# An encoder block in one program: the first norm's place in the engines' queues, weight rounding among bank copies, and a new cycle of weight-tile offsets

## The chip, the core and the metric

The kernel runs on one core of a Trainium2 chip. The core has a matrix engine (TensorE, PE in the profile; its weight loads are shown as PEld), a vector engine (VectorE, DVE), a scalar engine (ScalarE, ACT), GpSimd (POOL), and SyncE (SP), which here only issues transfers. Engines read and write the on-chip memory SBUF; TensorE adds up in PSUM, which has eight banks. Each engine takes its own instructions in order, and an instruction that needs another engine's result waits for a semaphore; what stands behind it waits too.

The metric is the device time of one execution in microseconds (us). The time before is 1913.99 us, the median of three runs (1913.49 to 1914.49).

## The reference

One layer on 256 tokens of width 2048, all in float32. Nine vectors (shift, scale and gate for three sublayers) come from one conditioning vector:

```
mod = silu(c) @ w_ada + b_ada;  sh1, sc1, gt1, sh2, ... = split(mod, 9)
h = h + 0.5 * gt1 * swiglu(rms_norm(h, g1) * (1 + sc1) + sh1, w1_gate, w1_up, w1_down)
qkv = (rms_norm(h, g2) * (1 + sc2) + sh2) @ w_qkv
h = h + gt2 * concat(rms_norm(natten(qkv)), rms_norm(dilated(qkv))) @ w_o
h = h + 0.5 * gt3 * swiglu(rms_norm(h, g3) * (1 + sc3) + sh3, w2_gate, w2_up, w2_down)
```

The two feed-forward parts have 5632 hidden columns. The mixing part has 16 heads of 128: eight with a 2-D neighbourhood, eight with three dilated windows.

## The kernel before, in words

Activations stand transposed: a tile has 128 of the 2048 features on the partitions and the 256 tokens along them. There are 16 such feature tiles, numbered k below.

**Weights.** All large weights are one stream of chunks of 128 x 1024 floats (0.5 MB), eight blocks of 128 x 128 in each, in the order in which TensorE needs them. A chunk is loaded into one of five raw buffers (`wraw`, tile `rw`). ScalarE rounds it to a reduced format (`wsplit`, tile `hiw`), and VectorE writes what the rounding left over (tile `low`). For each block TensorE then runs a pair of matmuls (`mm2`): the rounded weight against the activation's rounded part and its remainder together (512 columns), and the weight's remainder against the rounded part (256 columns). `hiw` and `low` have four buffers each, taken in turn. A buffer is 1024 + 64 floats long, and the constant `PLACE` says at which offset, counted in floats, chunk number n lies in it: entry n modulo 8 has the offset of `hiw` and that of `low`. The number n counts every chunk of the stream. The chunks of `w_qkv` lie at (0, 0) whatever `PLACE` says.

**The nine vectors.** `w_ada` is read in 144 pieces of 1 MB (tiles `ra` and `rx`, three buffers), and VectorE reduces each against silu(c) to one column of a vector (L144, 2.3 us). These pieces are spread over the kernel: `bg_step` issues one and uses an earlier one, and the weight stream calls it at a set number of pieces per chunk (`RA`, `RB` and so on).

**The start.** VectorE and TensorE spread silu(c) over the partitions (tiles `dg`, `pc`, `cb`), the squares of x are summed over the features by matmuls against ones (`sq1`, `pstat`), and `rstd_from` turns the sum into the norm's factor r by a logarithm, an exponential and one step of refinement. For each of the first K1 = 6 feature tiles, the scale and shift pieces are reduced, VectorE multiplies (`nt`), and ScalarE adds the shift, once in full float32 (`xf`) and once rounded (`nx`).

**The split part.** For these six feature tiles and the first eight hidden tiles (NF0), the weights (twelve chunks, `w1_s`) aren't split: TensorE multiplies them in full float32 against `xf` (L470), each of eight results in a bank of its own (`pa`). When a bank is complete, ScalarE copies it to SBUF (`park`, L348). Then `up_first` runs the remaining 24 hidden tiles over the same six feature tiles with split chunks (`w1_a`, 36 chunks), adding two halves on ScalarE and VectorE (L343, L344). The rest of the layer follows: `w1_b`, the down projections, attention, and the second feed-forward part.

**Order.** A recording layer places the instructions of ScalarE, VectorE and SyncE by its own estimate of when each can run; `tc.high_priority(offset=...)` moves what is written under it ahead in that choice, and `after` asks that one instruction stand behind another without a wait. TensorE's order is nearly that of the program text.

Of the kernel before, what the change touches and what calls it, by code (L numbers as in the profile page):

```python
# [9 lines left out]
F32 = mybir.dt.float32  # L10
F32R = mybir.dt.float32r
AF = mybir.ActivationFunctionType
ALU = mybir.AluOpType
AX = mybir.AxisListType

P = 128
S = 256
D = 2048
# [5 lines left out]
EPS = 1e-6  # L24
NEG = -1e30
CW = 1024
K1 = 6
# [21 lines left out]
URGENT = 400  # L49
SOON = 60  # L50
LINE = 16
PLACE = ((12, 36),) + 3 * ((16, 0),) + ((44, 40),) + 3 * ((48, 0),)
MANUAL = {mybir.EngineType.PE}


# [10 lines left out]
def build(tc, a):  # L66
    nc = tc.nc
    with ExitStack() as ctx:
        cp = ctx.enter_context(tc.tile_pool(name="cp", bufs=1))
# [4 lines left out]
        def psum_pool(kind):  # L74

            if "cm" in pools:
                pools.pop("cm").__exit__(None, None, None)
            if kind:
                pools["cm"] = tc.tile_pool(name=f"p{kind}", bufs=4 if kind == "pair" else 8,
                                           space=bass.MemoryType.PSUM, reuse_waits="tile")  # L80
                pools["p"] = pools["cm"].__enter__()
# [4 lines left out]
        def bank(nm):  # L86
            return pools["p"].tile([P, 512], F32, tag="b", name=nm)
# [2 lines left out]

        ones = cp.tile([P, P], F32, name="ones")
        nc.vector.memset(ones, 1.0)
        epst = cp.tile([P, 1], F32, name="epst")
        nc.vector.memset(epst, EPS)
        ident = cp.tile([P, P], F32, name="ident")
        make_identity(nc, ident)

# [4 lines left out]
        h4 = [cp.tile([P, 4, S], F32, tag=f"h{k}", name=f"h{k}") for k in range(4)]  # L102
# [11 lines left out]

        queue = []
        lows = []
        late = []

        def after(ins, other, why):
            tc.add_manual_dep(  # L120
                ins.ins, other.ins.name,
                mybir.DependencyInfo(mybir.DependencyClass.NoSync, mybir.DependencyReason.DATA),
                reason=why)
# [30 lines left out]
        def wraw(src):  # L154
            raw = wp.tile([P, CW], F32, tag="raw", bufs=RAWB, name="rw")
            ins = nc.sync.dma_start(raw, src)
            if ws.rate:
                queue[:] = [ins]
            return raw

        def wsplit(raw, place):
            hi = wp.tile([P, CW + 64], F32R, tag="whi", bufs=LOB, name="hiw")[:, place[0] : place[0] + CW]
            lo = wp.tile([P, CW + 64], F32R, tag="wlo", bufs=LOB, name="low")[:, place[1] : place[1] + CW]
            nc.scalar.copy(hi, raw)  # L164
            lows[:] = lows[-1:] + [nc.vector.tensor_tensor(lo, raw, hi.bitcast(F32), ALU.subtract)]  # L165
            return hi, lo

# [21 lines left out]
        def ln_exp_set():  # L189
            tc.keep_in_program_order(nc.scalar.preload_act_table_set("natural_log_exp_and_others"))  # L190

        def rstd_from(ps, n, w, tag):
            t0 = sp.tile([P, w], F32, tag="sq", name=f"{tag}0")
            t1 = sp.tile([P, w], F32, tag="nt", name=f"{tag}1")
            r = sp.tile([P, w], F32, tag=f"{tag}r", bufs=2, name=f"{tag}r")
            nc.scalar.activation(t0, ps, AF.Ln, scale=1.0 / n, bias=epst)
            nc.vector.tensor_scalar(t1, ps, -0.5 / n, -0.5 * EPS, ALU.mult, ALU.add)
            nc.scalar.activation(r, t0, AF.Exp, scale=-0.5)
            nc.vector.tensor_tensor(t0, r, r, ALU.mult)
            nc.vector.tensor_tensor(t0, t0, t1, ALU.mult)  # L200
            nc.vector.scalar_tensor_tensor(r, t0, 1.5, r, ALU.add, ALU.mult)
            return r

        class Stat:
# [25 lines left out]
            def rstd(self, n, tag="rs"):  # L230
                return rstd_from(self.ps, n, S, tag)

        def norm_mod(k, r, jsh, jsc, full=None):
            sh, gs = mods[jsh], mods[jsc]
            t = sp.tile([P, S], F32, tag="nt", name="nt")
            nc.vector.scalar_tensor_tensor(t, h[k], gs[:, k : k + 1], r, ALU.mult, ALU.mult)
            if full is not None:
                nc.scalar.activation(full, t, AF.Identity, bias=sh[:, k : k + 1])
            nc.scalar.activation(nx[k][:, 0, :], t, AF.Identity, bias=sh[:, k : k + 1])  # L239
            return nc.vector.scalar_tensor_tensor(  # L240
                nx[k][:, 1, :], t, sh[:, k : k + 1], nx[k][:, 0, :].bitcast(F32), ALU.add, ALU.subtract)
# [13 lines left out]
        def bg_use():  # L255
            raw, i, then = pend.pop(0)
            ada_use(raw, i)
            if then:
                then()

        def bg_step():
            i, then = bg.pop(0)
            while len(pend) >= (ARA + ARX - 1 if wide else ARA - 1):
                bg_use()
            pend.append((ada_issue(i), i, then))

        def bg_until(left):

            while len(bg) + len(pend) > left:
                if bg:  # L270
                    bg_step()
                else:
                    bg_use()
# [11 lines left out]
        srcs = []  # L285
        first = {}
        for nm in ("w1_s", "w1_a", "w1_b", "w1_d", "w1_c", "w1_e", "w_qkv", "w_o",
                   "w2_a", "w2_b", "w2_d", "w2_c", "w2_e"):
            first[nm] = len(srcs)
            for c in range(a[nm].shape[0]):  # L290
                srcs.append((a[nm][c], (0, 0) if nm == "w_qkv" else PLACE[len(srcs) % len(PLACE)]))

        class W:
# [8 lines left out]
            def fetch(self, n):  # L302
                while self.head < n:
                    self.ready[self.head] = wraw(srcs[self.head][0])
                    self.head += 1

            def whole(self):
                self.tail += 1
                return self.ready.pop(self.tail - 1)

            def chunk(self, ahead=AHEAD):
                while self.head <= min(self.tail + ahead, len(srcs) - 1):
                    self.ready[self.head] = wsplit(wraw(srcs[self.head][0]), srcs[self.head][1])
                    self.head += 1
                    self.credit += self.rate
                    while self.credit >= 1.0 and (bg or pend):
                        self.credit -= 1.0
                        if bg:
                            bg_step()
                        else:  # L320
                            bg_use()
                self.tail += 1
                return self.ready.pop(self.tail - 1)
# [13 lines left out]
        ws = W()  # L337
# [7 lines left out]

        def park(ps, f, part):
            part[f] = hp.tile([P, 2, S], F32, tag="hid", name=f"pt{f}")
            nc.scalar.copy(part[f], ps)  # L348

        def up_mm(ps, k0, k1, first, last):  # L350
            for j in range(2):
# [75 lines left out]
        part = {}  # L427
# [15 lines left out]
        ps1 = bank("pstat")[:, :S]  # L443
        for q in range(4):
            for i in range(2):
                sq = hp.tile([P, 2, S], F32, tag="hid", name="sq1")
                nc.scalar.activation(sq, h4[q][:, 2 * i : 2 * i + 2, :], AF.Square)
                nc.vector.tensor_tensor(sq[:, 0, :], sq[:, 0, :], sq[:, 1, :], ALU.add)
                nc.tensor.matmul(ps1, ones, sq[:, 0, :], start=q + i == 0, stop=q + i == 4)
        r1 = rstd_from(ps1, D, S, "rs")  # L450

        def first_full(k):
            full[k] = hp.tile([P, 2, S], F32, tag="hid", name=f"xf{k}")[:, 0, :]
            norm_mod(k, r1, 0, 1, full[k])

        full = {}
        for k in range(K1):
            bg_add((KT + k, k), lambda k=k: first_full(k))
        bg_pairs(K1, r1, 0, 1)
        pa = [bank(f"pa{f}").rearrange("p (j s) -> p j s", j=2) for f in range(NF0)]  # L460
        bg_step()
        bg_step()
        for k in range(K1):
            ws.fetch(2 * k + 2)
            bg_until((KT - 1 - k) * 2)
            for j in range(2):
                w = ws.whole()
                for b in range(8):
                    f, q = 4 * j + b // 2, b % 2
                    nc.tensor.matmul(pa[f][:, q, :], w[:, b * P : (b + 1) * P], full[k],  # L470
                                     start=k == 0 and q == 0, stop=k == K1 - 1 and q == 1,
                                     skip_group_check=True)
        for f in range(NF0):
            park(pa[f], f, part)
        psum_pool("pair")

        ws.pace(RA)
# [36 lines left out]
        with tc.tile_pool(name="att", bufs=2) as ap_, tc.tile_pool(name="atc", bufs=1) as ac:  # L514
# [41 lines left out]
            def qk_rstd(s_):  # L556
                s_["rr"] = rstd_from(s_["ss"], HD, 8, "rq")
# [197 lines left out]
        part = {}  # L755
# [103 lines left out]
def _program():  # L859
    import concourse.bacc as _bacc  # L860

    nc = _bacc.Bacc("TRN2", target_bir_lowering=False, num_devices=1, dynamic_dma_scratch_size=1024)
    aps = {k: nc.dram_tensor(f"in_{k}_dram", s, F32, kind="ExternalInput").ap() for k, s in _SHAPES.items()}
    aps["out"] = nc.dram_tensor("out_0_dram", (KT, P, S), F32, kind="ExternalOutput").ap()
    with tile.TileContext(nc) as tc:
        build(tc, aps)
    return nc
# [10 lines left out]
```

## Time and profile before

| What | Value |
|---|---|
| median of three timed runs | 1913.99 us |
| the profiled execution's own time | 1911.73 us |
| its span in the trace | 1910.0 us |
| TensorE busy | 1876.7 us, 98% |
| weight loads busy | 1633.8 us, 86% |
| VectorE busy | 1563.4 us, 82% |
| ScalarE busy | 907.5 us, 48% |
| granted TensorE clock, mean | 0.996 |
| read from HBM | 500.09 MB, 263 GB/s over the span |

The span runs from the first to the last instruction of the program; 1.7 us of the profiled execution lie around it. The busy share of TensorE says how long matmuls were under way and not how closely they follow each other, so the prediction also uses the length of stretches that hold a known number of matmuls. Times below are microseconds from the start of the span.

### The profile page before, as it was taken

What the parts mean: (1) busy time and instruction counts of PE and PEld (TensorE: products, weight loads), DVE (VectorE), ACT (ScalarE), POOL (GpSimd) and SP (SyncE); (2) the same over time, 40 slices, a digit from 0 to 9 for tenths busy, and PEclk for the clock granted to TensorE, in tenths of its full rate; (3) what the DMA queues carried; (4) which work ended last, traced back from release to release, by engine and by line L of the source; (5) the groups of instructions that cost most, each with busy time, mean ns of one, the idle gap of its engine ahead of it and who ended that gap; (6) DMA issues with size and microseconds to landing.
All of it is one profiled execution on the core that took longest, in us unless ns stands there. A gap on an engine that the chain in (4) does not pass through costs nothing.

```text
span 1910.0 us, 27533 instructions
## 1 busy us (share of the span) xinstructions
PE 1876.7 (98%) x10564; PEld 1633.8 (86%) x10564; DVE 1563.4 (82%) x2122; ACT 907.5 (48%) x1333; POOL 0.7 (0%) x6
## 2 busy tenths in 40 slices
PE   7999999999999999999999999999999999999999
PEld 5878888888888888888888888888888888888888
DVE  7899999988888889878887898888699985556565
ACT  2444544443334454555555555454555543334442
POOL 0000000000000000000000000000000000000000
PEclk8999999999999999999999999999999999999999
DMA  9988888889898987777765444888677876666664
GB/s 384 387 326 293 306 296 303 298 316 331 330 334 322 328 307 262 253 258 251 253 230 193 147 153 161 314 297 304 209 280 258 276 272 216 192 193 193 189 207 134
DMA packets 120227, 503.98 MB, mean 264 GB/s; under 512 B 13344, under 2 KB 15904, under 8 KB 101664
## 3 DMA queue, kind: packets, MB, share of 16 engines
q1 hardware_dynamic: 120096, 502.24, 75.4%
q8 instruction: 82, 1.34, 0.3%
q14 instruction: 49, 0.40, 0.1%
HBM read 500.09 MB, written 2.10 MB: 263 GB/s over the span
## 4 chain that ended last, share of the span: by engine, by line
PE 92%; DVE 5%; ACT 1%; DMA 1%; issue 1%; SPq 0%; ACTq 0%; DVEq 0%
PE pb L170 23%; PE pd L170 17%; PE pb L171 12%; PE pd L171 8%; PE pa L170 8%; PE pqk L176 5%; PE pqq L176 5%; PE pa L171 4%; PE pqv L176 4%; PE pa L470 2%; PE pso L170 2%; DVE low L165 2%; PE pso L171 1%; DVE ra L144 1%; DMA ra<-in_w_ada_dram 1%
## 5 line engine op out<-in xcount | busy, mean ns | idle before, releaser
L164 ACT CAST hiw<-rw 128x1024 fp32r<-128x1024 f32 x644 | 674.3, 1050 | 726.3 <-PE pd L170 241.7
L165 DVE TENSOR_TENSOR low<-rw,hiw 128x1024 fp32r<-128x1024 f32 x644 | 785.5, 1222 | 271.4 <-ACT hiw L164 269.8
L170 PE MATMUL pb<-nx,hiw 128*128 128x512 f32 x1920 | 656.8, 390 | 0.0
L171 PE MATMUL pb<-nx,low 128*128 128x256 f32 x1920 | 531.6, 277 | 0.7 <-DVE low L165 0.7
L170 PE MATMUL pd<-hd,hiw 128*128 128x512 f32 x1408 | 481.5, 390 | 0.0
L170 PEld LDWEIGHTS pb<-nx,hiw 128*128 128x128 f32 x1920 | 360.4, 188 | 76.6
L171 PE MATMUL pd<-hd,low 128*128 128x256 f32 x1408 | 389.6, 277 | 0.0
L171 PEld LDWEIGHTS pb<-nx,low 128*128 128x128 f32 x1920 | 360.5, 188 | 1.2 <-DVE low L165 1.2
L170 PEld LDWEIGHTS pd<-hd,hiw 128*128 128x128 f32 x1408 | 264.3, 188 | 56.2
L170 PE MATMUL pa<-nx,hiw 128*128 128x512 f32 x800 | 276.2, 392 | 4.7 <-ACT hiw L164 3.2
L171 PEld LDWEIGHTS pd<-hd,low 128*128 128x128 f32 x1408 | 264.3, 188 | 0.0
L144 DVE CUSTOM_DVE_ANT_0 ra<-ra,cb,vec 128x2048 f32<-128x2048 f32 x101 | 236.9, 2345 | 4.9 <-DMA ra<-in_w_ada_dram 4.9
L171 PE MATMUL pa<-nx,low 128*128 128x256 f32 x800 | 221.5, 279 | 3.9 <-DVE low L165 3.8
L170 PEld LDWEIGHTS pa<-nx,hiw 128*128 128x128 f32 x800 | 149.5, 188 | 38.5 <-ACT hiw L164 5.2
L171 PEld LDWEIGHTS pa<-nx,low 128*128 128x128 f32 x800 | 150.3, 188 | 8.8 <-DVE low L165 7.8
L144 DVE CUSTOM_DVE_ANT_0 rx<-rx,cb,vec 128x2048 f32<-128x2048 f32 x43 | 100.9, 2346 | 1.2 <-DMA rx<-in_w_ada_dram 1.2
L170 PE MATMUL pso<-ox,hiw 128*128 128x512 f32 x256 | 90.9, 399 | 0.0
L176 PE MATMUL pqk<-hiw,nx 128*128 128x512 f32 x256 | 84.3, 395 | 0.0
L176 PE MATMUL pqq<-hiw,nx 128*128 128x512 f32 x256 | 83.0, 393 | 0.0
L176 PE MATMUL pqv<-hiw,nx 128*128 128x512 f32 x256 | 81.4, 392 | 0.3 <-ACT nx L239 0.3
L385 DVE SCALAR_TENSOR_TENSOR h<-pd,m,h 128x256 f32<-128x256 f32 x128 | 60.8, 481 | 20.2 <-PE pd L171 18.3
L171 PE MATMUL pso<-ox,low 128*128 128x256 f32 x256 | 71.8, 280 | 0.0
(133 smaller groups left out, 1504.2 us busy)
## 6 DMA issues: line engine op xcount, KB each, us to landing
ra<-in_w_ada_dram SPq DMA_DIRECT2D x101, 1024.0 KB, 7.0
rw<-in_w_b_dram SPq DMA_DIRECT2D x144, 512.0 KB, 4.5
rw<-in_w_d_dram SPq DMA_DIRECT2D x128, 512.0 KB, 4.4
rw<-in_w_a_dram SPq DMA_DIRECT2D x100, 512.0 KB, 4.7
rw<-in_w_c_dram SPq DMA_DIRECT2D x96, 512.0 KB, 4.3
rw<-in_w_qkv_dram SPq DMA_DIRECT2D x96, 512.0 KB, 3.9
rx<-in_w_ada_dram SPq DMA_DIRECT2D x43, 1024.0 KB, 7.5
rw<-in_w_e_dram SPq DMA_DIRECT2D x48, 512.0 KB, 4.6
```

Of the source, the lines that this page charges most:

```text
L144: ins = nc.vector.tensor_tensor_reduce(out=raw, in0=raw, in1=cb, scale=1.0, scalar=vec[:, BA + i : BA + i + 1], op0=ALU.mult, op1=ALU.add, ...
L164: nc.scalar.copy(hi, raw)
L165: lows[:] = lows[-1:] + [nc.vector.tensor_tensor(lo, raw, hi.bitcast(F32), ALU.subtract)]
L170: nc.tensor.matmul(out, lh, r, start=first, stop=False)
L171: nc.tensor.matmul(out[:, :S], ll, r[:, 0, :], start=False, stop=last)
L176: nc.tensor.matmul(out, l, r, start=first and i == 0, stop=last and i == 2, **kw)
L385: nc.vector.scalar_tensor_tensor(h[d], part_, g, h[d], ALU.mult, ALU.add)
L470: nc.tensor.matmul(pa[f][:, q, :], w[:, b * P : (b + 1) * P], full[k], start=k == 0 and q == 0, stop=k == K1 - 1 and q == 1, skip_group_ch ...
```

## The change

There are three parts, and nothing else in the program differs.

First, the norm at the start. The squares of the last quarter of x are computed by VectorE and no longer by ScalarE. In `rstd_from`, called with `on_act`, two steps of the refinement (the linear term and the square of r) move from VectorE to ScalarE. The norm's factor and the first feature tile's `nt`, `xf` and `nx` are written under high priority.

Second, the first chunks of `w1_a`. Two of them are loaded (`early`) before the two `w_ada` pieces that the last round of the split part issues, and all that concerns their rounding is written (`fill`) ahead of the bank copies, with the fourth and the seventh copy set behind the first and the second cast.

Third, `PLACE`. Before: (12, 36), then three times (16, 0), then (44, 40), then three times (48, 0). Now: (44, 40), then seven times (48, 0).

```diff
-PLACE = ((12, 36),) + 3 * ((16, 0),) + ((44, 40),) + 3 * ((48, 0),)
+PLACE = ((44, 40),) + 7 * ((48, 0),)
...
-            nc.scalar.copy(hi, raw)
+            casts[:] = casts[-1:] + [nc.scalar.copy(hi, raw)]
...
+            if on_act:
+                nc.scalar.activation(r, t0, AF.Exp, scale=-0.5)
+                nc.scalar.activation(t1, ps, AF.Identity, scale=-0.5 / n, bias=epsh)
+                nc.scalar.activation(t0, r, AF.Square)
+            else:
...
+            def early(self, n):
+                self.raws = [wraw(srcs[self.head + i][0]) for i in range(n)]
+
+            def fill(self):
+                for raw in self.raws:
+                    self.ready[self.head] = wsplit(raw, srcs[self.head][1])
+                    self.head += 1
...
-                nc.scalar.activation(sq, h4[q][:, 2 * i : 2 * i + 2, :], AF.Square)
+                xs = h4[q][:, 2 * i : 2 * i + 2, :]
+                if q < 3:
+                    nc.scalar.activation(sq, xs, AF.Square)
+                else:
+                    nc.vector.tensor_tensor(sq, xs, xs, ALU.mult)
...
-        r1 = rstd_from(ps1, D, S, "rs")
+        with tc.high_priority(offset=URGENT):
+            r1 = rstd_from(ps1, D, S, "rs", True)
...
-            norm_mod(k, r1, 0, 1, full[k])
+            with tc.high_priority(offset=URGENT if k == 0 else 0):
+                norm_mod(k, r1, 0, 1, full[k])
...
             ws.fetch(2 * k + 2)
+            if k == K1 - 1:
+                ws.early(2)
...
+        casts.clear()
+        ws.fill()
         for f in range(NF0):
-            park(pa[f], f, part)
+            ins = park(pa[f], f, part)
+            if f in (3, 6):
+                after(ins, casts[f // 3 - 1], "cast")
```

VectorE at the first norm, before. Rows of this kind name a line of the kernel, the operation, what is written and read, and the size; two ISA rows are one reduction of a `w_ada` piece, `m` is a column of one of the nine vectors, `rs` and `rsr` are the tiles of `rstd_from`. The first row is the tail of the first reduction (`ra_195`).

```order
L144 ISA m_88 128x1
L448 TENSOR_TENSOR sq_174<-sq_174 128x256
L152 SCALAR_TENSOR_TENSOR m_88<-m_88,vec 128x1
L144 ISA rx_197,m_87<-rx_197,cb,vec 128x2048
L144 ISA m_87 128x1
L197 TENSOR_SCALAR rs_179<-pstat 128x256
L199 TENSOR_TENSOR rs_178<-rsr 128x256
L200 TENSOR_TENSOR rs_178<-rs_178,rs_179 128x256
L201 SCALAR_TENSOR_TENSOR rsr<-rs_178,rsr 128x256
L144 ISA ra_205,m_88<-ra_205,cb,vec 128x2048
L144 ISA m_88 128x1
L236 SCALAR_TENSOR_TENSOR nt<-h_78,m_88,rsr 128x256
```

The same place now:

```order
L467 TENSOR_TENSOR sq_175<-h_82 128x512
L468 TENSOR_TENSOR sq_175<-sq_175 128x256
L147 ISA ra_196,m_89<-ra_196,cb,vec 128x2048
L147 ISA m_89 128x1
L147 ISA rx_198,m_88<-rx_198,cb,vec 128x2048
L147 ISA m_88 128x1
L208 TENSOR_TENSOR rs_179<-rs_179,rs_180 128x256
L155 SCALAR_TENSOR_TENSOR m_89<-m_89,vec 128x1
L209 SCALAR_TENSOR_TENSOR rsr<-rs_179,rsr 128x256
L244 SCALAR_TENSOR_TENSOR nt<-h_79,m_89,rsr 128x256
L147 ISA ra_206,m_89<-ra_206,cb,vec 128x2048
```

The last addition of squares moved ahead of both reductions, two steps of the refinement are gone from VectorE, and the first `nt` moved ahead of the third reduction.

ScalarE at the end of the split part, before (`pt` and `pa` are the copies and the eight banks):

```order
L348 COPY pt_397<-pa_187 128x512
L348 COPY pt_399<-pa_188 128x512
L348 COPY pt_401<-pa_189 128x512
L348 COPY pt_403<-pa_190 128x512
L348 COPY pt_405<-pa_191 128x512
L348 COPY pt_407<-pa_192 128x512
L348 COPY pt_409<-pa_193 128x512
L348 COPY pt_411<-pa_194 128x512
L164 CAST hiw<-rw 128x1024
L239 ACTIVATE nx_102<-nt,m_87 128x256
L164 CAST hiw<-rw 128x1024 x2
```

Now:

```order
L364 COPY pt_410<-pa_188 128x512
L364 COPY pt_412<-pa_189 128x512
L167 CAST hiw<-rw 128x1024
L364 COPY pt_414<-pa_190 128x512
L167 CAST hiw<-rw 128x1024
L364 COPY pt_416<-pa_191 128x512
L364 COPY pt_418<-pa_192 128x512
L364 COPY pt_420<-pa_193 128x512
L364 COPY pt_422<-pa_194 128x512
L364 COPY pt_424<-pa_195 128x512
L167 CAST hiw<-rw 128x1024
L359 COPY pt_477<-pa 128x512
```

Two of the casts now stand behind the second and the third bank copy. On VectorE, the two matching `low` instructions now stand behind the last `nx` of the split part and ahead of the reductions of the seventh feature tile's two pieces (`ra_375`, `rx_384`); before, the first `low` stood behind both of these reductions.

SyncE's issues behind the last two chunks of the split part, before:

```order
L135 DMA ra_370<-in_w_ada_dram 128x2048
L135 DMA rx_379<-in_w_ada_dram 128x2048
L156 DMA rw<-in_w_a_dram 128x1024 x3
L135 DMA ra_438<-in_w_ada_dram 128x2048
L156 DMA rw<-in_w_a_dram 128x1024 x2
```

Now:

```order
L159 DMA rw<-in_w_a_dram 128x1024 x2
L138 DMA ra_375<-in_w_ada_dram 128x2048
L138 DMA rx_384<-in_w_ada_dram 128x2048
L159 DMA rw<-in_w_a_dram 128x1024 x3
L138 DMA ra_467<-in_w_ada_dram 128x2048
```

The first two chunks of `w1_a` moved ahead of two 1 MB pieces, and each later piece stands two chunks further back. From the beginning of `w1_b` on, the order on every engine is the same as before.

More of the change, by code (lines that the diff above doesn't have):

```diff
@@ L92, in build @@
         nc.vector.memset(ones, 1.0)
-        epst = cp.tile([P, 1], F32, name="epst")
+        eps2 = cp.tile([P, 2], F32, name="epst")
+        epst, epsh = eps2[:, 0:1], eps2[:, 1:2]
         nc.vector.memset(epst, EPS)
+        nc.vector.memset(epsh, -0.5 * EPS)
         ident = cp.tile([P, P], F32, name="ident")
@@ L116, in build @@
         lows = []
+        casts = []
         late = []
@@ L190, in ln_exp_set, with rstd_from @@
             tc.keep_in_program_order(nc.scalar.preload_act_table_set("natural_log_exp_and_others"))
-        def rstd_from(ps, n, w, tag):
+        def rstd_from(ps, n, w, tag, on_act=False):
             t0 = sp.tile([P, w], F32, tag="sq", name=f"{tag}0")
@@ L196, in rstd_from @@
             nc.scalar.activation(t0, ps, AF.Ln, scale=1.0 / n, bias=epst)
-            nc.vector.tensor_scalar(t1, ps, -0.5 / n, -0.5 * EPS, ALU.mult, ALU.add)
-            nc.scalar.activation(r, t0, AF.Exp, scale=-0.5)
-            nc.vector.tensor_tensor(t0, r, r, ALU.mult)
+            if on_act:
[3 more added lines that the diff above has]
+            else:
+                nc.vector.tensor_scalar(t1, ps, -0.5 / n, -0.5 * EPS, ALU.mult, ALU.add)
+                nc.scalar.activation(r, t0, AF.Exp, scale=-0.5)
+                nc.vector.tensor_tensor(t0, r, r, ALU.mult)
             nc.vector.tensor_tensor(t0, t0, t1, ALU.mult)
@@ L347, in park @@
             part[f] = hp.tile([P, 2, S], F32, tag="hid", name=f"pt{f}")
-            nc.scalar.copy(part[f], ps)
+            return nc.scalar.copy(part[f], ps)
         def up_mm(ps, k0, k1, first, last):
```

## The prediction

> **What bounds the kernel now.** I read the chain of waits first, then stretches of the span, then the timelines of the first 70 us. By the chain, TensorE carries the span:
>
> ```profile
> PE 92%; DVE 5%; ACT 1%; DMA 1%; issue 1%; SPq 0%; ACTq 0%; DVEq 0%
> ```
>
> Stretches (length, then busy time with instruction count of PE, PEld, DVE, ACT and POOL, granted clock, DMA share, GB/s) show where it doesn't:
>
> ```profile
> 22.60:66.12 43.52, 43.49 (x192) 37.64 (x192) 31.48 (x39) 9.02 (x18) 0.00 (x0) 0.96 1.01 407
> ...
> 66.12:177.16 111.04, 103.91 (x578) 87.18 (x577) 103.11 (x119) 52.68 (x70) 0.00 (x0) 1.00 0.90 338
> 177.16:200.27 23.11, 22.40 (x130) 19.38 (x129) 17.96 (x19) 12.63 (x14) 0.00 (x0) 1.00 0.79 276
> 200.27:640.00 439.73, 439.73 (x2575) 388.40 (x2574) 397.36 (x492) 197.99 (x241) 0.00 (x0) 1.00 0.87 315
> ```
>
> The split part (22.6 to 66.1) is full on TensorE and on the DMA engines at once. The `w1_a` part loses 7.1 us of TensorE time, `w1_b` 0.7 us at its beginning, and from 200 us TensorE is gapless for a long time. So a shift that survives until 200 us reaches the end, and in the gapless parts only the matmuls' own pace counts. The chain through the start, in order of time:
>
> ```profile
> 19.28 2.35 DVE ra L144
> ...
> 21.64 0.41 DVE nt L236
> ...
> 22.07 0.52 ACT xf L238
> ...
> 22.63 43.51 PE pa L470 x192
> 66.14 0.02 issue
> 66.16 0.58 ACT pt L348
> 66.75 0.95 ACT hiw L164
> 67.70 0.02 issue
> 67.72 1.24 DVE low L165
> 68.96 0.04 issue
> 69.00 0.39 PE pa L171
> ```
>
> The first `nt` waits for a reduction of the next feature tile, and behind the split part TensorE waits for the eighth bank copy, one cast and one `low`.
>
> **Part 1, the first norm.** VectorE's timeline:
>
> ```profile
> 8.16 1.46 DVE L448 TENSOR_TENSOR sq<-sq 128x256 f32<-128x256 f32 x3 [0.58 <-ACT sq L447]
> ...
> 10.74 0.42 DVE L448 TENSOR_TENSOR sq<-sq 128x256 f32<-128x256 f32 x1 [1.12 <-ACT sq L447]
> 11.86 2.35 DVE L144 CUSTOM_DVE_ANT_0 ra<-ra,cb,vec 128x2048 f32<-128x2048 f32 x1 [0.70 <-DMA ra<-in_w_ada_dram]
> 14.14 0.08 DVE L144 DVE_READ_ACCUMULATOR2_ANT m<- 128x1 f32 x1
> ...
> 17.60 0.43 DVE L200 TENSOR_TENSOR rs<-rs,rs 128x256 f32<-128x256 f32 x1
> 18.06 0.42 DVE L201 SCALAR_TENSOR_TENSOR rsr<-rs,rsr 128x256 f32<-128x256 f32 x1
> ```
>
> The first six additions are over at 9.62. Two squares and two additions are left. A square of 128x512 on VectorE isn't in the trace; its bounds are 0.42 (the 256-column addition) and 1.22 (the 1024-column `low` on the page), and I take 0.65, nearer the lower for its size. Four instructions make 2.1 us, so the first reduction starts at about 11.9 to 12.2 (its piece is there at 11.86). Two reductions at 2.28 from start to start (11.86 to 14.14) end at 16.4 to 16.8. The refinement's last two steps at 0.46 each and `nt` follow, and from `nt` to the first matmul the chain has 0.99 us (21.64 to 22.63). That gives 18.4 to 18.8; with a few tenths for the small instruction between them, **18.9**, 3.7 us earlier. ScalarE's two added steps cost the path nothing: the last square is added by 12.2, one small matmul and four steps at 0.51 each (the `xf` row below, of the same size) end about 15, while VectorE reduces until 16.4. Without that cover the two would cost 1.0. If the last quarter of x came late, the square on VectorE would hold up both reductions queued behind it; ScalarE began on that quarter by 10.1 at the latest, since the addition at 10.74 follows its 0.6 us square, and this is the 12.2 above.
>
> How much of 3.7 is left at 66.12? Two limits stand in these rows (the granted clock is the third figure from the end):
>
> ```profile
> 22.62:26.28 3.66, 3.65 (x9) 2.90 (x10) 3.08 (x5) 1.27 (x3) 0.00 (x0) 0.50 1.03 425
> 26.28:31.20 4.92, 4.92 (x24) 4.34 (x23) 4.40 (x6) 0.00 (x0) 0.00 (x0) 1.00 0.99 370
> 59.20:66.12 6.92, 6.92 (x33) 5.75 (x31) 4.24 (x6) 4.10 (x7) 0.00 (x0) 1.00 1.01 412
> 66.12:69.10 2.98, 0.59 (x3) 0.28 (x2) 1.38 (x2) 2.94 (x5) 0.00 (x0) 1.00 0.94 335
> ...
> 55.99 0.51 ACT L238 ACTIVATE xf<-nt,m 128x256 f32<-128x256 f32 x1 [6.62 <-DVE m L144]
> ```
>
> The sixth feature tile takes TensorE 6.92 us and began at 59.20; moved by 3.7 it would begin at 55.5. But its `xf` ends at 56.5, and that hangs on a `w_ada` piece behind a DMA stream at a share of 1.0, which nothing here makes earlier. So the split part ends at 56.5 + 6.9 = 63.45, **2.6 us earlier**. The other limit: the first 3.65 us ran at half clock. If the cold stretch is as long again, the DMA stream decides. If it is twice as long, half of the added 3.65 is lost, 1.8 us: the last tile begins at 57.3, the part ends at 64.2, and 1.9 are left. Bounds: 1.9 to 2.7.
>
> The Trainium skill speaks against counting on the first case: "TensorE: Matmul & The Clock Gate", section "What's actually happening", says that the clock opens after one busy window of about 3.4 us and that this window runs freely, so an earlier first matmul can fall badly in it. The rows agree with one window (3.65 us at 0.50); by the rule alone the cold time lies anywhere between one and two windows, and at worst the sum would be 0.7 us smaller.
>
> **Part 2, casts among the copies.** Row 66.12:69.10 has 0.59 busy of 2.98: 2.4 us are lost there. With the part ending at 63.45, the first two copies (at -6.0 and -5.1 us from its end, see below) are over at 58.9, the first cast at 60, its `low` at 61.2, the second `low` at 62.6: both in time.
>
> ```profile
> 60.12 0.58 ACT L348 COPY pt<-pa 128x512 f32<-128x512 f32 x1 [3.22 <-PE pa L470]
> 60.98 0.59 ACT L348 COPY pt<-pa 128x512 f32<-128x512 f32 x1 [0.28 <-PE pa L470]
> 61.84 0.59 ACT L348 COPY pt<-pa 128x512 f32<-128x512 f32 x1 [0.28 <-PE pa L470]
> ```
>
> The casts need their chunks by then. They move ahead of two pieces of 1 MB, 2.5 us of stream each at 412 GB/s, and so land 5 us earlier than before. The bank copies come up to 1.9 us later (two casts), into the 0.28 us gaps between copies; no matmul waits, since four pairs of banks are taken in turn.
>
> On SyncE the second of these chunks waits for a raw buffer that TensorE still reads, and the two pieces queue behind it:
>
> ```profile
> SPq L156 <- PE pa L470: 28.0, 10, 5.6
> ```
>
> Ten such waits sum to 28.0, 2.8 each. The pieces belong to the seventh feature tile, which TensorE first reads in `w1_b`, a hundred microseconds later: no cost.
>
> What is late next is the third `low`: behind the two lows VectorE has two reductions, ending near 67.8, and the third `low` near 69.1, where TensorE wants it at 63.45 + 2 x 2.72 + 0.2 = 69.1. I take **2.1** of 2.4 (bounds 1.5 and 2.4).
>
> **Does it last to 200 us?** In the `w1_a` part:
>
> ```profile
> ACT pt L343 <- PE pa L171: 52.0, 21, 3.5
> PEld pa L171 <- DVE low L165: 6.7, 11, 1.1
> ```
>
> ScalarE waits in 21 places for TensorE's results, the casts stand behind these copies, the lows behind the casts: the waits form a loop that begins with TensorE and so moves with it. VectorE's 103.1 us of work there shrink by two lows (2.4) and one reduction that the pacing moves out (2.3) and fit into the earlier stretch. I carry all 4.7; bounds 0 (VectorE holds its old end) and 5.2.
>
> **Part 3, the offsets.** Chunk by chunk in the down projection (PE rows only; starts of eight pairs):
>
> ```profile
> 397.19:399.98 2.79, 2.79 (x19) 1.00 0.99 367
> 399.98:402.70 2.72, 2.72 (x19) 1.00 0.79 238
> ...
> 408.14:410.91 2.77, 2.77 (x19) 1.00 0.83 245
> 410.91:413.63 2.72, 2.72 (x19) 1.00 0.86 276
> ```
>
> A chunk at (12, 36) takes 2.79, at (44, 40) 2.77, at (16, 0) and (48, 0) 2.72. Eight chunks take 2.79 + 2.77 + 6 x 2.72 = 21.88 and would take 2.77 + 7 x 2.72 = 21.81: 0.07 us less, within 0.01 of rounding. Of the 548 chunks outside `w_qkv` I leave out the 36 of `w1_a` and the 32 of the output projection, where waits set the pace: 480 chunks, 60 cycles, 3.6 to 4.2. I take **3.7**, near the lower end, since waits also lie at the beginning of the second feed-forward part (bounds 3.0 and 4.2).
>
> The offsets also bear on how long a slow pace lasts. After a stall in the output projection the pace is slow at unchanged offsets until (44, 40) comes:
>
> ```profile
> 1131.29:1134.09 2.80, 2.80 (x18) 1.00 0.53 190
> ...
> 1139.69:1142.53 2.84, 2.84 (x18) 1.00 0.65 185
> ...
> 1145.27:1147.99 2.72, 2.72 (x18) 1.00 0.51 193
> ```
>
> So a slow pace persists, and (12, 36) just ahead of these did not end it. Both cycles have one (44, 40) in eight, so I expect no more slow chunks than before.
>
> **Sum.** 2.6 + 2.1 + 3.7 = 8.4. The profiled execution took 1911.73, hence 1903.3; the median is 2.26 above that execution, hence **1905.6**.
>
> **Rivals.** (a) *Only the stall goes*: the early start is eaten by clock or stream. For it: DMA share 1.0 throughout; against: TensorE was gapless, so it was TensorE that was late. 2.1 + 3.7: 1908.2. Chance 0.12. (b) *The buffer, not the offset, is slow*: before, odd offsets only ever fell on the first of four buffers, so the trace can't tell the two apart. Then only 2.79 to 2.77 is won, 0.9 us: 1908.4. Chance 0.12. (c) *VectorE holds the `w1_a` part*: 103.1 of 111.0 us busy speaks for it, the loop against it. Only 3.7 remain: 1910.3. Chance 0.07. (d) *Slower*: seven equal chunks in a row let the slow pace come back at the wrap from the fourth buffer to the first, where today an odd chunk always stands, and it then lasts to the next (44, 40). A slow cycle is 2.84 + 7 x 2.80 = 22.44, against 21.81 in the forecast and 21.88 today. At 0.63 us each, 14 of the 60 cycles eat the 8.4; with half of them slow the time is 1924.5, with all 1943. Against it: from 200 to 640 us 2575 matmuls are 161 chunks, which at today's 21.88 for eight make 440.2, and 439.7 were taken, so no chunk there left the fast pace by itself. Chance 0.07. The forecast has 0.62.
>
> About 0.2%, 3.8 us, is what a measurement here tells from no change: faster means under 1910.2, slower over 1917.8. Forecast, (a) and (b) are faster, with a little taken off for their upper ends: 0.84; same 0.09; slower 0.07. The likeliest range by itself is 1903.5 to 1908; with (a), (b) and half of (c), 1902 to 1911.
>
> **What would show it.** First full-precision matmul at 18.9 and not 22.6; its part ending near 63.5; no gap of a microsecond behind it; `w1_b` beginning near 172.5 where it began at 177.2; in the down projection, chunks of 2.77, then seven of 2.72. The prediction is wrong if the fifth chunk of a cycle stays at 2.77, if 2.80 spreads beyond stalls, or if `w1_b` begins at 175 or later.

## The result and the profile after

| | before | after |
|---|---|---|
| median, runs taken in turn (range) | 1913.74 us (1912.26 to 1914.49, 4 runs) | 1902.70 us (1902.06 to 1903.51, 4 runs) |
| ratio, 95% interval | | 0.9946 (0.9931 to 0.9961) |
| median, a later series (range) | 1912.65 us (1912.24 to 1914.29, and one run of 4887.58) | 1903.01 us (1900.70 to 1903.33, 5 runs) |
| ratio of that series | | 0.9946 (0.9933 to 0.9959) |
| the profiled execution / its span | 1911.73 / 1910.0 us | 1902.98 / 1901.2 us |

The run of 4887.58 us was in a slow state and is left out of the ratio. The ratios, here and below, are estimates over the runs and not the quotients of the medians. The kernel is faster by 9.6 to 11.0 us by medians, by 8.75 by profiled executions. The forecast was 1905.6, with 8.4 us won.

The page of after, its first group and the engine line of its chain of waits:

```profile
PE 1873.3 (99%) x10564; PEld 1633.8 (86%) x10564; DVE 1563.3 (82%) x2123; ACT 907.4 (48%) x1333; POOL 0.7 (0%) x6
...
PE 89%; DVE 6%; DMA 2%; ACT 1%; issue 1%; SPq 0%; ACTq 0%; DVEq 0%
```

TensorE's share of the chain fell from 92% to 89%, though TensorE is still the bound: the start of the chain now runs through other work. Its first 57 us, in order of time:

```profile
9.26 0.69 DVE sq L467
...
11.94 2.34 DVE ra L147
14.29 2.31 DVE rx L147
16.63 10.17 DMA rx<-in_w_ada_dram
...
40.12 10.20 DMA rx<-in_w_ada_dram
50.34 2.35 DVE rx L147
...
55.72 0.52 ACT xf L246
56.27 7.17 PE pa L494 x32
```

Before, one TensorE entry of 43.51 us stood here, from 22.63 on. Now three transfers of `w_ada` pieces and the reductions behind them lead to the `xf` of the sixth feature tile, and TensorE joins only for that tile, at 56.27. Two engines' timelines show the moved work (start, length, engine, line):

```profile
10.87 0.69 DVE L467 TENSOR_TENSOR sq<-h 128x512 f32<-128x512 f32 x1
...
17.43 0.48 DVE L244 SCALAR_TENSOR_TENSOR nt<-h,m,rsr 128x256 f32<-128x256 f32 x1
```

```profile
58.79 1.05 ACT L167 CAST hiw<-rw 128x1024 fp32r<-128x1024 f32 x1
59.73 0.59 ACT L364 COPY pt<-pa 128x512 f32<-128x512 f32 x1
60.21 1.06 ACT L167 CAST hiw<-rw 128x1024 fp32r<-128x1024 f32 x1
```

The first `nt` stands at 17.43 where it stood at 21.56 in the same view, and both casts are over before the split part ends. Stretches of after (length; busy time with count of PE, PEld, DVE, ACT, POOL; granted clock; DMA share; GB/s):

```profile
18.50:23.56 5.06, 5.05 (x12) 4.06 (x13) 4.24 (x6) 0.36 (x1) 0.00 (x0) 0.50 1.02 414
18.50:63.45 44.95, 44.54 (x193) 38.19 (x194) 32.56 (x39) 10.39 (x20) 0.00 (x0) 0.94 1.02 414
63.27:171.31 108.04, 102.54 (x578) 87.39 (x577) 102.40 (x120) 50.67 (x68) 0.00 (x0) 1.00 0.92 351
```

The split part runs from 18.5 to 63.45 and TensorE waits 0.4 us in it. `w1_b` begins at 171.31, 5.85 us earlier than before. The same for TensorE alone (length, PE busy, clock, DMA share, GB/s), first before, from the end of the split part through the first split chunk, and the `w1_b` part; then after, and behind them chunks 0, 1 and 4 of a cycle in the down projection:

```profile
66.12:71.66 5.54, 3.15 (x18) 1.00 0.96 362
177.16:397.19 220.03, 219.32 (x1282) 1.00 0.83 293
```

```profile
63.45:66.18 2.73, 2.73 (x17) 1.00 1.02 392
171.31:391.38 220.07, 218.85 (x1283) 1.00 0.83 295
391.38:394.15 2.77, 2.77 (x19) 1.00 0.97 389
394.15:396.87 2.72, 2.72 (x19) 1.00 0.69 229
...
402.31:405.03 2.72, 2.72 (x19) 1.00 0.86 252
```

The gap behind the split part is gone, and the fifth chunk of a cycle (402.31) takes 2.72 like its neighbours.

### The profile page after: what moved, and what is told of

It is laid out like the page before. It is cut to its first block, busy times and chain, and to the rows that moved or that the text cites. A ratio compares the mean times of both kernels' runs of the same rounds, so it can differ in the third digit from the quotient of the medians.

```text
span 1901.2 us, 27533 instructions
## 1 busy us (share of the span) xinstructions
PE 1873.3 (99%) x10564; PEld 1633.8 (86%) x10564; DVE 1563.3 (82%) x2123; ACT 907.4 (48%) x1333; POOL 0.7 (0%) x6
## 4 chain that ended last, share of the span: by engine, by line
PE 89%; DVE 6%; DMA 2%; ACT 1%; issue 1%; SPq 0%; ACTq 0%; DVEq 0%
PE pb L173 23%; PE pd L173 17%; PE pb L174 11%; PE pa L173 9%; PE pd L174 8%; PE pqk L179 5%; PE pqq L179 5%; PE pa L174 4%; PE pqv L179 4%; DVE low L168 2%; DMA rx<-in_w_ada_dram 2%; PE pso L173 1%; DVE rx L147 1%; DVE ra L147 1%; PE pso L174 1%
```

## The experiments

Each group of runs had runs of before on the same chip: their medians were 1912.51, 1913.06 and 1912.65 us.

**The parts alone.** In `e1_norm_alone` the casts and the offsets are as before, in `e2_casts_alone` the norm and the offsets, in `e3_offsets_alone` all but `PLACE`; `e4_both_starts` has everything but `PLACE`.

```diff
 e1, against before
+                if q < 3:
+                    nc.scalar.activation(sq, xs, AF.Square)
+                else:
+                    nc.vector.tensor_tensor(sq, xs, xs, ALU.mult)
...
+        with tc.high_priority(offset=URGENT):
+            r1 = rstd_from(ps1, D, S, "rs", True)
...
+            with tc.high_priority(offset=URGENT if k == 0 else 0):
+                norm_mod(k, r1, 0, 1, full[k])
 e2, against before
+            if k == K1 - 1:
+                ws.early(2)
...
+        ws.fill()
...
+            if f in (3, 6):
+                after(ins, casts[f // 3 - 1], "cast")
 e3, against before; e4 is after with the first of these lines for the second
-PLACE = ((12, 36),) + 3 * ((16, 0),) + ((44, 40),) + 3 * ((48, 0),)
+PLACE = ((44, 40),) + 7 * ((48, 0),)
```

> The first norm's part alone, on the kernel before. Theory (the split part is held by TensorE's late start up to what the DMA stream allows, and the stages behind it move with it): first full-precision matmul at 18.5 to 18.9, split part ending at 63.5 and not 66.1, the gap behind the eighth bank copy unchanged at 2.4 us, so about 2.6 us less than the kernel before. Rival (the early start is eaten by the half-rate clock or the stream): no more than 0.5 us less. Open: the timed runs of the whole change gained 11.0 us where its trace accounts for 8.8; if the 2.2 belong to the start, this kernel gains about 4.8 in the timed runs.

> The casts among the bank copies, with the two chunks loaded earlier, alone on the kernel before. Theory: the split part still ends at 66.1, the gap behind it goes from 2.4 us to under 0.3, and about 2.1 to 2.4 us less in all. Rival (VectorE holds the stage that follows): the gap goes, but the w1_b part begins where it began, 177.2, and the time is the same within 0.5 us.

> The cycle of offsets alone on the kernel before. Theory (pace is set by the offset): 3.0 to 3.7 us less; in the down projection one chunk of 2.77 and seven of 2.72. Rival (the first of four buffers is slow at any offset): 0.9 us less, the fifth chunk of a cycle at 2.77.

> The norm and the casts together, with the offsets of the kernel before. Theory (the parts add up): the gains of the two alone, 4.7 to 5.9 us, w1_b beginning at 171.3 to 172.5. Rival (VectorE holds the stage between): under 2 us.

| run | median (range) | ratio, 95% interval | saved |
|---|---|---|---|
| norm alone | 1909.68 (1908.38 to 1912.71) | 0.9991 (0.9982 to 1.0000) | 2.8 |
| casts alone | 1908.60 (1906.94 to 1911.64) | 0.9980 (0.9971 to 0.9988) | 3.9 |
| offsets alone | 1907.37 (1907.06 to 1910.61) | 0.9978 (0.9969 to 0.9986) | 5.1 |
| norm and casts | 1906.53 (1905.69 to 1906.97) | 0.9970 (0.9958 to 0.9981) | 6.0 |

The 28 runs of before in this group lay between 1910.50 and 1914.16. A single part isn't measured better than within 1.7 us by its time: by the ratios the four saved 1.7, 3.8, 4.2 and 5.7 us. The medians of e2, e3 and e4 saved more than was expected (3.9 for at most 2.4, 5.1 for 3.7, 6.0 for 5.9), within these intervals. So the traces have to say more. TensorE's rows of e1, from the first full-precision matmul:

```profile
18.70:63.78 45.08, 44.70 (x192) 0.94 1.02 417
63.78:65.40 1.62, 0.00 (x1) 1.00 0.97 400
```

The early norm alone ends the split part at 63.78, and the gap behind it stays. `w1_b` begins at 174.88, 2.3 us earlier than before. Rows of e2, then of e3, which start as late as before:

```profile
22.58:28.28 5.70, 5.70 (x13) 0.50 1.02 421
22.58:66.91 44.33, 44.33 (x193) 0.94 0.96 381
```

```profile
22.43:27.66 5.23, 5.22 (x12) 0.50 1.02 423
22.43:66.71 44.28, 44.27 (x192) 0.94 1.00 402
178.02:397.39 219.37, 218.66 (x1283) 1.00 0.83 293
```

The casts alone close the gap: matmuls follow each other from 22.58 through 66.91. `w1_b` begins at 175.13, although the split part ended later than in the trace of before. For that, these rows show a reason that the prediction didn't use for the late start: the half-clock stretch was 5.70 and 5.22 us long, not 3.65. With the late start each of its microseconds beyond 3.65 costs about half a microsecond (66.9 and 66.7 against 66.1). The profiled execution of before had met a short one. The last row is the `w1_b` part with the new cycle: 0.66 us less for 80 chunks, 0.066 for a cycle. Both starts together:

```profile
18.36:21.60 3.24, 3.23 (x8) 0.50 0.98 402
18.36:62.96 44.60, 43.65 (x193) 0.96 1.02 414
```

`w1_b` began at 171.10 in e4, against 171.31 in after and 177.16 before. That is 6.1 us earlier, no less than the 2.3 of e1 and the 2.0 of e2 together (e2's execution had lost 0.8 to its longer half-clock stretch). So rival (a), in which the early start is eaten, falls.

**Clock or DMA stream?** Two kernels keep the clock full ahead of the split part. The added matmuls have results that nobody reads.

```diff
 e8: after, e10: before
         bg_pairs(K1, r1, 0, 1)
+        idle(18)        # idle(30) in e10
```

> The changed kernel with 18 added 128x128 matmuls whose results nobody reads, between the sums of squares and the first full-precision matmul, so that TensorE is busy there and its clock is not halved. Theory: with the earlier first norm the DMA stream sets the end of the split part (its sixth feature tile waits for its last piece), not the clock; the clock is full at 18.5, the part still ends at 63.2 to 63.8, TensorE's wait ahead of the sixth tile grows from 0.65 to about 3 us, and the time stays 1902.7 within 0.5. Rival: the clock sets it; the part ends 2.5 us earlier, near 61, and the time is 1900.2.

> The kernel of before with 30 added 128x128 matmuls whose results nobody reads, ahead of the first full-precision matmul, so that the clock is full when it starts at 22.6. Theory: with the late start it is the half clock that sets the end of the split part; of a cold stretch of 3.65 to 5.7 us (the traces so far) half is won, the part ends at 64.2 in place of 66.1 to 67.1, the time is 2 to 3 us below the median of before, near 1910, and the runs spread over 2.5 us instead of 3.7. Rival: the DMA stream sets the end there too; then the part ends at 66 and the time stays within 0.5 us of before.

TensorE's rows of e8, then of e10:

```profile
13.90:18.30 4.40, 4.23 (x37) 1.00 1.04 426
18.34:63.68 45.34, 42.85 (x193) 1.00 1.02 412
33.40:41.46 8.06, 7.18 (x33) 1.00 1.02 419
```

```profile
15.30:22.60 7.30, 6.70 (x61) 1.00 1.01 416
22.60:64.35 41.75, 41.71 (x192) 1.00 1.02 417
64.35:65.97 1.62, 0.01 (x1) 1.00 1.04 377
```

In e8 nothing ran at half clock, and yet the part ended at 63.68: TensorE waited 2.5 us (45.34 less 42.85), in several feature tiles and not only ahead of the sixth (one took 8.06 in place of 6.91). The time was 1902.63 us (1902.23 to 1902.90; ratio 0.9945, 0.9933 to 0.9957), that of after. So with the early norm the DMA stream ends the split part, and a full clock gains nothing. The margin is small. In the trace of e9 (described below; its split part has the instructions of after's) the first matmul stood only at 19.19 and 6.12 us ran at half clock. There TensorE had no wait, its chain of waits has it in one entry as before's has, and the part ended at 63.90, 0.45 later than in after:

```profile
19.19:25.31 6.12, 6.12 (x14) 0.50 1.02 418
19.19:63.90 44.71, 44.71 (x193) 0.93 1.01 407
```

In e10, with the late norm, the same full clock ended it at 64.35, 1.8 us earlier than in the trace of before, gapless. The time was 1910.87 us (1910.04 to 1912.99; ratio 0.9992, 0.9983 to 1.0000): 1.8 below before's median, where 2 to 3 were expected, and the runs spread over 3.0 us, no less than before's in the same group. The place of the gain is shown by the rows; its size in the time only within 0 to 3.3 us.

**The changed kernel again.**

> The changed kernel again, so that more of its runs stand beside more of before's. Theory: its runs keep within 2 us (1902 to 1904), while before's spread over 3.5 us, since its split part ends with the DMA stream whatever the clock does; median 1902.7. Rival: the four runs so far agreed by chance; then they spread over 3.5 us as well, with a median up to 1904.

Median 1903.01, from 1900.70 to 1903.33: the nine runs of after spread over 2.8 us, not over 2. The median of the first four was no accident; that its runs agree better than before's is not shown.

**What the odd chunk is for.** The new cycle keeps one odd chunk, (44, 40), of 2.77 us. The prediction said that a slow pace persists until such a chunk ends it. Three kernels change only the offsets of after:

```diff
 e5 and e11 (the same kernel twice)
+PLACE = 8 * ((48, 0),)
 e7
+PLACE = ((12, 36),) + 7 * ((48, 0),)
 e9
-PLACE[len(srcs) % len(PLACE)]
+PLACE[len(srcs) % len(PLACE) if len(srcs) <= 56 or 360 <= len(srcs) <= 400 else 1]
```

> The changed kernel with all eight places at (48, 0), no odd chunk. Theory: a slow pace (350 ns for a pair, 2.80 us for a chunk) that a stall leaves behind lasts until an odd chunk ends it. Without one, each of the two long stretches without a stall (212 chunks of the first feed-forward part, 264 of the second) is all fast or all slow, as its last stall left it: 60 x 0.05 = 3.0 us are won, and 212 x 0.08 = 17 or 264 x 0.08 = 21 are lost where it is slow. So the time is one of about 1899.7, 1917, 1921 and 1938, and it may differ by such steps from run to run. Rival: the slow pace ends by itself (at the wrap of the four buffers, or after a few chunks); then 1899.7, within 1.5 us in all runs.

> The changed kernel with its odd chunk at (12, 36) instead of (44, 40). Theory: what ends a slow pace is (44, 40) alone, since in the trace of before a chunk at (12, 36) was followed by slow chunks in the output projection; then long slow stretches appear, as without an odd chunk, and the time is 1917 or more in some or all runs. Rival: any other place ends it; then only 2.79 instead of 2.77 for one chunk in eight, 60 x 0.02 = 1.2 us: 1903.9.

> The changed kernel with its odd chunk (44, 40) only up to the chunk 56 and from 360 to 400, where TensorE has stalls; all others at (48, 0). Theory: a slow pace begins only at a stall, so the odd chunks elsewhere cost 0.05 us each and do nothing: 52 of them less, 2.6 us, 1900.1. Rival: the slow pace begins now and then by itself; then slow stretches appear between 200 and 1060 us or behind 1200 us, each chunk 0.08 longer, and the time is over 1903.

> The kernel without an odd chunk again, beside the changed kernel on the same chip. If the slow pace can last through the long stretches where a stall leaves it, some of these runs are 17 or 21 us longer than 1899; if the last stall before each stretch always leaves the fast pace, as in its five runs so far, all are 1897 to 1901 and 3.0 us under the changed kernel.

| run | median (range) | ratio, 95% interval |
|---|---|---|
| no odd chunk, e5 | 1899.41 (1897.17 to 1900.39) | 0.9927 (0.9915 to 0.9940) |
| no odd chunk, e11 | 1899.95 (1898.92 to 1901.24) | 0.9933 (0.9919 to 0.9947) |
| (12, 36) as the odd chunk, e7 | 1904.86 (1903.61 to 1905.29) | 0.9955 (0.9942 to 0.9969) |
| odd only near stalls, e9 | 1898.94 (1897.87 to 1900.02) | 0.9926 (0.9914 to 0.9939) |

None of the ten runs without an odd chunk was 17 us too long, so the loss that the theory priced did not come. That a slow pace persists is shown all the same, in the output projection. TensorE's rows of e11, then of e5 and of e9, each from the first or second chunk behind the same stall on:

```profile
1120.79:1123.77 2.98, 2.98 (x19) 1.00 0.09 33
1123.77:1126.57 2.80, 2.80 (x19) 1.00 0.62 187
1126.57:1162.97 36.40, 36.40 (x211) 1.00 0.60 188
1162.97:1165.77 2.80, 2.80 (x18) 1.00 0.61 189
...
1184.80:1187.52 2.72, 2.72 (x19) 1.00 0.61 193
```

```profile
1120.71:1123.44 2.73, 2.73 (x19) 1.00 0.53 192
1123.44:1158.80 35.36, 35.36 (x211) 1.00 0.61 188
...
1181.48:1826.12 644.64, 644.64 (x3795) 1.00 0.75 245
```

```profile
1120.28:1123.24 2.96, 2.96 (x19) 1.00 0.07 29
1123.24:1125.96 2.72, 2.72 (x19) 1.00 0.64 193
```

The same thirteen chunks at the same offsets took 36.40 in one execution of one kernel and 35.36 in another: 2.80 a chunk against 2.72, with nothing waiting. In e11 the slow pace lasted for fifteen chunks up to the next stall; in e9, where (44, 40) stands right behind the stall, the next chunk was fast. But behind the stalls at the beginning of the second feed-forward part both executions were fast, e5 for all 237 chunks (644.64 / 2.72) up to 1826 us. Why that stall leaves the fast pace each time, and whether it always does, stays open. So the odd chunk can be worth something near stalls, 1.2 us in e11 (15 x 0.08), and nothing elsewhere, where leaving it out saves 60 x 0.05 = 3.0 us. The medians of both kernels that leave it out there are 3 to 4 us below the changed one's. The intervals of the ratios overlap, so the reading rests on the 2.72 of the chunks in the rows as much as on the times; the runs don't tell e9 from e5.

For e7, the long slow stretches that were expected didn't come. A chunk at (12, 36) and the one behind it, first after a stall, then in the down projection:

```profile
74.72:77.50 2.78, 2.78 (x19) 1.00 1.04 429
77.50:80.30 2.80, 2.80 (x19) 1.00 1.00 382
391.75:394.54 2.79, 2.79 (x19) 1.00 0.93 367
394.54:397.27 2.73, 2.73 (x19) 1.00 0.81 255
```

Once the slow pace went through (12, 36) into the next chunk (77.50). Behind a fast cycle it costs 2.79 and 0.01 in the chunk behind, 0.03 more for a cycle than (44, 40): 60 x 0.03 = 1.8, and the median lay 1.9 to 2.2 above after's. The price of the cycle is about as large as that difference, which the interval (2.6 us either way) doesn't resolve; that (44, 40) alone ends a slow pace is not shown, since behind most stalls of e7 the pace was fast again without it.

## Why the prediction was right, point by point

**First matmul at 18.9.** It began at 18.52. The square on VectorE took 0.69 where 0.65 was taken, and the first reduction began at 11.94, within the forecast 11.9 to 12.2. ScalarE's two added steps were covered.

**The split part's end at 63.45.** It ended there to the hundredth in after, and between 63.14 and 63.91 in the eight other traces with the early norm. The hundredth is luck: the `xf` of the sixth tile ended at 56.23 where 56.5 was taken, and its matmuls took 7.17 us where 6.9 was taken. The reason held: e8 shows that the stream decides. The cold stretch was longer than before's (5.05 against 3.65 us at 0.50). The other limit of the prediction, half of the added cold time, came to bear in one trace of the nine, e9. The Trainium skill's "TensorE: Matmul & The Clock Gate", section "What's actually happening", says that the clock opens after at least one busy window of about 3.4 us and that this window runs freely, from which the prediction took a cold time of one to two windows. The traces agree roughly, with 3.2 to 6.1 us in the rows above. The 0.7 us that the page's rule could have cost the early start was hidden by the stream, but for the 0.45 of e9; it is the late starts that pay.

**Casts among the copies, 2.1.** Mis-sized, too small. The first split chunk ended 5.54 us behind the split part before, 2.73 after: 2.8 were won. The row that gave 2.4 counts idle time alone, and these are its two waits (before, TensorE):

```profile
67.74 0.50 PE L170 MATMUL pa<-nx,hiw 128*128 128x512 f32 x1 [1.62 <-ACT hiw L164]
69.00 0.39 PE L171 MATMUL pa<-nx,low 128*128 128x256 f32 x1 [0.77 <-DVE low L165]
```

The next matmul stood at 69.23. So this pair cost 0.50 and 0.23 us beside the waits, where a pair in a gapless row takes 0.34, and that is the missing 0.4. The third `low`, which I had at 69.1, ended at 68.9 and was in time.

**Does it last to 200 us?** Yes. Two starts gave 5.5 us at the end of the first split chunk and 5.85 at `w1_b`, where 4.7 was carried; the loop from TensorE's results to ScalarE's copies moved along, and rival (c) falls. Of that, 0.7 us didn't reach the end: `w1_b`'s third chunk, which holds a stall, took 3.56 us where it took 2.87, and the `w1_b` part is as long as before (220.07 against 220.03) in spite of the new cycle. This belongs to the casts: the chunk took 3.51 to 3.56 us in all nine traces with the early casts and 2.87 to 3.06 in the four without. The prediction had put the two `w_ada` pieces that now load later down at no cost; what holds the chunk was not traced.

**The offsets, 3.7.** Chunks of 2.77 and seven of 2.72 came as forecast. The pace of the 480 chunks counted gave 4.1 by the traces (summed over their gapless pairs, 6.88 us above 340 ns for a pair before, 2.76 after). The output projection, which was left out, gained a little: in all five traces with the old cycle its second to fourth chunks took 2.80, in all eight with a new one 2.72 or 2.73. Rival (b) falls with the fifth chunk's 2.72, and (d) because no slow chunk appeared away from the start and the stalls.

**The sum.** Between the two profiled executions the account closes: 5.85 us at `w1_b`, less the 0.7, with the 4.1 of the offsets, less 0.5 in the output projection (114.95 us against 114.49; at half clock after ran twice in it, before once) make the 8.8 by which the spans differ. Yet the median, 1902.70, lies inside the wide range (1902 to 1911) and below the likeliest one (1903.5 to 1908). Here is the step that failed: "the median is 2.26 above that execution, hence 1905.6". The 2.26 was added as if it were a constant of the measurement. It was the luck of one execution of before and of three of its runs: the profiled execution of after lay within 0.3 us of its median, those of the experiments between 2.2 below (e5) and 3.0 above (e2), and before's median in the later groups was 0.8 to 1.3 above 1911.73. With 1.0 in its place the same terms give 1904.3. What is left, 1.3 to 1.6 us, is of the size of two things that the sum lacked: 0.6 for the half-clock stretch that a late start meets (4.9 us in the mean of before, e2 and e3, against 3.65, halved), which the early start no longer pays, and the 0.7 by which the casts were too small. Three traces of a late start can't settle these shares, so they are argued, not shown. The half clock late in the kernel (last section) is a rival for a part of them: the output projection took 113.37 us (e1) to 115.79 (e2) in the traces with the old offsets, so before's 114.49 was a draw too.

## What to carry to other kernels

Before pricing an earlier start, ask which of two parallel limits ends the stage: here the clock ended it before and the DMA stream after (but for e9), and 18 and 30 dummy matmuls told the two apart in one kernel each. Take the difference between one profiled execution and a median for what it is, a draw, and look in the trace for what was drawn (a half-clock stretch of 3.65 us that is 5 us elsewhere). Offsets of weight tiles in SBUF are worth trying one by one, over thousands of gapless pairs: 0.05 us for a chunk was 3 us in the whole.

## What the hardware did that was not expected

A pair of matmuls (512 and 256 columns) has two steady paces at the same offsets, 340 and 350 ns, and a stall decides which: fifteen chunks at 2.80 and the same at 2.72 in e11 and e5, with nothing waiting in either. Which part of the path sets the phase is not known from these runs.

The half clock also comes back late in the kernel, and not in every execution. The output projection as a whole, in after and in e3 (TensorE's rows):

```profile
1060.93:1175.88 114.95, 107.86 (x649) 0.97 0.53 165
```

```profile
1066.92:1180.15 113.23, 106.12 (x649) 0.98 0.51 168
```

Both have a wait of 3.0 us in attention near their beginning. After it, after ran for 3.4 us at 0.50, and e3 didn't (a later stretch, at the end of these rows, both have): 1.7 us of difference between kernels that are the same there, as large as a part of the change. All half-clock stretches in the traces, the waits inside them included, lasted 3.4, 6.8 or 10.2 us, but for the last of each trace, which the end of the kernel cuts.
